# Layer norm sums all on VectorE in PSUM, four squares in flight, half of the float32 modulated tiles of 512 columns in a PSUM bank

## The chip, the cores and the metric

The kernel runs on one core of a Trainium2 chip. A core has five engines with queues of their own: TensorE (PE in the profile, its weight loads PEld), VectorE (DVE), ScalarE (ACT), GpSimd (POOL) and SyncE (SP, here only for DMAs). Each engine works through its queue in order. Data lies in SBUF, and in PSUM, which has eight banks of 512 float32 columns on 128 partitions; the engines that compute here read and write both, but GpSimd works on SBUF alone in this kernel. The metric is the time of one execution in device microseconds (us). Less is better.

## The reference

A two-layer backbone over 512 latent tokens and 256 context tokens of width 1024. Each layer is a half SwiGLU feed-forward, a mixer (neighbourhood attention in layer 0, windowed attention in layer 1) and a second half SwiGLU. Each of these sub-layers is modulated at its input and closed by a layer norm:

```python
def layer_norm(x, g, b):
    xf = x.astype(jnp.float32)
    mu = jnp.mean(xf, axis=-1, keepdims=True)
    var = jnp.mean(jnp.square(xf - mu), axis=-1, keepdims=True)
    return ((xf - mu) * lax.rsqrt(var + LN_EPS)).astype(x.dtype) * g + b

def modulate(h, shift, scale):
    return h * (1.0 + scale) + shift

def ffn_sublayer(h, shift, scale, gate, w_in, w_out, g, b):
    y = swiglu(modulate(h, shift, scale), w_in, w_out)
    return layer_norm(ALPHA * h + FFN_RES * gate * y, g, b)
```

## The kernel before

**Layout.** The hidden state lies transposed: the 1024 features are eight tiles `z[d]` of 128 partitions, the tokens are columns (0 to 511 latent, 512 to 767 context). A mean over features is then a sum over the eight tiles and over partitions.

**Precision.** Every float32 operand of the large matmuls is split into a high part and a rest (`uh`, `ul` for the modulated state, `wh`, `wl` for weights, `gh`, `gl` for the gated activations), and each product is three matmuls (`mm3`, lines 146 to 148). ACT rounds the weights to `wh` (line 102), POOL subtracts to get `wl` (line 104).

**Order.** The program is written as a sequence of tile operations. A planner orders each engine's queue by modelled times (`schedule_with_timeline_sim=True`), finds the dependencies between tiles, and hands out buffers: a tile with a tag takes one of the tag's `bufs` slots when its last user has finished. So PE's queue is a mixture of stages, and a matmul that stands in the queue ahead of others holds them back if its operand is late.

**PSUM.** `banks` gives the eight banks out by tag: "mm", "s" and "c" two each, "t" and "o" one each.

**Layer norm.** `layer_norm` (line 385) handles one group of columns, 256 or 512 wide. The groups are named by their key and place: l0_0 and l0_1, l2_0 and l2_1, l3_0 and l3_1 (each time 512 latent columns, then 256 context columns), l1_0, l1_1, l1_2 (256 each), l4_0, l4_1 (256 each), fin_0 (256). The last group of the program, fin_1, uses `layer_norm_pe`, which sums by matmuls. The steps of `layer_norm` are:

1. Sum of the eight tiles (`total` as `as..`): POOL adds tiles 0 to 3 into a SBUF tile, three adds; DVE adds tiles 4 to 6 into `part`, then POOL's sum, then tile 7, four adds.
2. A matmul with a matrix of 1/1024 sums over partitions and gives the mean `pm` to every partition (line 393).
3. DVE centers each tile in place (`center`, line 333), ACT squares it (line 398). Squares 0 to 2 are summed on POOL (two adds), square 3 is written to `part`, and DVE adds 4 to 7 and POOL's sum (five adds). Squares that don't start a sum go to the tag "ln" with two buffers.
4. Matmuls give the variance `pv` (line 404), eleven small DVE operations give its inverse root (`rstd`), a matmul spreads it over partitions (`spread`, line 356).

`pm`, `pv` and `spread` use one bank tag. `part` is the second half of `pm`'s own bank for a group of 256 columns, and the bank "t" for a group of 512.

**After the norm.** `ln_mod` multiplies each tile by the inverse root (line 411) and calls `mod_out`, which makes the modulated tile in float32 (`uf`, line 287, ACT), its high part (`uh`, line 289 on ACT or line 291 on DVE) and the rest (`ul`, line 292, DVE). For 512 columns `uf` takes one of the twelve "slab" buffers, which also hold weights and attention operands. `keep` (lines 299 and 305, POOL) then scales the tile for the residual. Group l3_0 reads and writes through a rearranged view of the columns (`rm`).

**Feed-forward tail.** `ffn` runs its chunks so that the latent group `a` is finished first. In the last chunk (`ci == NCH - 1`) come the products of `a`, then those of group `b` and the layer norm of `a` (`post(0)`), then `down` of `b`; the chunk marked "r" repeats the one before for `b` alone, with another `down` of `b`. `down` (line 466) makes eight products `pd` of six matmuls each, and DVE accumulates each into `z` (`accumulate`, line 432). In the tail `down` takes its banks from "sst" in turn: two of "s" and the one of "t".

Of the kernel before, what the change touches and what calls it, by code (L numbers as in the profile page):

```python
# [8 lines left out]
F32 = mybir.dt.float32  # L9
# [9 lines left out]
P = 128  # L19
D = 1024  # L20
DT = D // P
# [5 lines left out]
NCH = NF // 2  # L27
# [4 lines left out]
SLABS = 12  # L32
# [6 lines left out]
def hybrid_kernel(ctx: ExitStack, tc: tile.TileContext, h0, cc, crow, wmod, wmodt, bmod, lnp, wst,  # L39
                  rpbp, nmask, sinks, ropec, rmat, ident, wmask, out):  # L40
    nc = tc.nc
# [8 lines left out]
    def bank(tag, nm):  # L50
        return pp.tile([P, 512], F32, tag=tag, name=nm, bufs=banks[tag])

    def t2(nm, tag="t2"):
        return tp.tile([P, 512], F32, tag=tag, name=nm, bufs={"t2": 6, "ln": 2, "sl": 2}[tag])
# [28 lines left out]
    def zt(d, c0, c1):  # L83
        return zl[d][:, c0:c1] if c1 <= NL else z[d][:, c0:c1]
# [24 lines left out]
    ph, phase_of = {}, [None, ExitStack()]  # L109
# [159 lines left out]
    def mod_out(nm, d, c0, c1, st, prm, rm=False, dd=None):  # L269

        sc, bi, ag, ab = prm
        dd = d if dd is None else dd
        n = c1 - c0
        zs = zt(d, c0, c1)
        s1, s2 = sc[:, dd, st:st + 1], bi[:, dd, st:st + 1]
        if nm == "in":
            uf = t2(f"uf{nm}_{d}", "ln" if d < 3 else "t2")
        elif nm == "l0_1":
            uf = gp.tile([P, 256], F32, tag="gs", name=f"uf{nm}_{d}", bufs=6)
        elif n <= 256:  # L280
            uf = ph["S"].tile([P, 256], F32, tag="v", name=f"uf{nm}_{d}", bufs=9)
        else:
            uf = ph["S"].tile([P, 512], F32, tag="slab", name=f"uf{nm}_{d}", bufs=SLABS)
        uo, uv, lo, zv = uh[d][:, c0:c1], uf[:, :n], ul[d][:, c0:c1], zs
        if rm:
            uo, uv, lo, zv = rowm(uo), rows(uv), rowm(lo), rows(zs)
        nc.scalar.activation(uf[:, :n], zs, AF.Identity, scale=s1, bias=s2)  # L287
        if d in (1, 2, 4, 5, 7):
            hi = nc.scalar.activation(uo, zv, AF.Identity, scale=s1, bias=s2)
        else:  # L290
            hi = nc.vector.tensor_scalar(out=uo, in0=zv, scalar1=s1, scalar2=s2, op0=ALU.mult, op1=ALU.add)  # L291
        return hi, nc.vector.tensor_tensor(out=lo, in0=uv, in1=uo.bitcast(F32), op=ALU.subtract)  # L292
# [23 lines left out]
    def add(eng, out, a, b):  # L316
        behind(eng.tensor_tensor(out=out, in0=a, in1=b, op=ALU.add), last_rstd[0])
# [18 lines left out]
    def total(nm, n, src, split, part):  # L336


        accs = [t2(f"{nm}_{i}")[:, :n] for i in range(2)]
        a = src(0, accs[0])  # L340
        for d in range(1, split):
            add(nc.gpsimd, accs[0], a, src(d, None))
            a = accs[0]
        a = src(split, part)
        for d in range(split + 1, DT):
            if d == DT - 1:
                add(nc.vector, part, a, accs[0])
            add(nc.vector, accs[1] if d == DT - 1 else part, a, src(d, None))
            a = part
        return accs[1]  # L350

    def spread(nm, y, n, tag):

# [31 lines left out]
    def layer_norm(nm, c0, c1, tag):  # L385

        n = c1 - c0
        nj = n // P
        bk = bank(tag, f"pm{nm}")
        pm = bk[:, 0:n]  # L390
        part = bk[:, 256:256 + n] if n <= 256 else bank("t", f"pp{nm}")[:]
        acc = total(f"as{nm}", n, lambda d, acc: zt(d, c0, c1), 4, part)
        nc.tensor.matmul(pm, onesd[:], acc, start=True, stop=True)

        def square(d, acc):
            zs = center(d, c0, c1, pm)
            sq = acc if acc is not None else t2(f"sq{nm}_{d}", "ln")[:, :n]
            nc.scalar.activation(sq, zs, AF.Square)
            return sq

        acc = total(f"aq{nm}", n, square, 3, part)
        pv = bank(tag, f"pv{nm}")
        for j in range(nj):
            x = nc.tensor.matmul(pv[:, j:j + 1], acc[:, j * P:(j + 1) * P], onesd[:, 0:1], start=True, stop=True)
            behind(x, prev_ln[0])
        ve = pv[:, 8:8 + nj]
        nc.vector.tensor_scalar(out=ve, in0=pv[:, :nj], scalar1=EPS, scalar2=None, op0=ALU.add)
        pr, prev_ln[0] = spread(nm, rstd(nm, ve, nj, pv[:, 16:16 + nj]), n, tag)

        def norm(d):  # L410
            return nc.vector.tensor_tensor(out=zt(d, c0, c1), in0=zt(d, c0, c1), in1=pr, op=ALU.mult)  # L411
        return norm
# [23 lines left out]
    def ffn(nm, groups, gt, mid, post, units=(), opened={}, head=None, apart=None):  # L436
# [25 lines left out]
        def next_bank(nm):  # L462
            turn[0] += 1
            return bank(("mm", "s", "c")[turn[0] % 3], nm)

        def down(w, ci, gs, g, spread):
            c0, c1, st = g
            for d in range(DT):
                pn = f"pd{nm}_{ci}_{c0}_{d}"
                pd = (next_bank(pn) if spread else bank("sst"[d % 3], pn))[:, :c1 - c0]  # L470
                for i in range(2):
                    mm3(pd, rw(w, i, d * P, (d + 1) * P), [t[:, c0:c1] for t in gs[i]], i == 0, i == 1)
                accumulate(pd, d, c0, c1, st, gts[0])
# [134 lines left out]
        for ci in list(range(NCH)) + [("r", NCH - 2)]:  # L608
            r = isinstance(ci, tuple)
            if not r and 0 < ci < NCH - 2:  # L610
                phase("T")
                pace[0] = each * weight[ci] / (4 if ci < s0 else 14)
                if ci == s0 - 1:
                    saved = sums()
            if not r and s0 <= ci < NCH - 2:
                gs = [[gp.tile([P, NT], F32R, tag="gs", name=f"g{x}{nm}_{ci}_{i}", bufs=6) for x in "hl"] for i in range(2)]

                def lagging(ci=ci, gs=gs, u=wpos[0] + 2):
                    w = wunit(again=u, adding=True)
                    if ci == NCH - 3:  # L620
                        restore(saved)
                    for g in ([(0, NL, 0)] if nb == 2 else groups):
                        down(w, f"{ci}", gs, g, True)

                for i in range(2):
                    seven(f"{nm}_{ci}_{i}", wpos[0] + i, *gs[i])
                    while i == 0 and late_downs:
                        late_downs.pop()()
                late_downs.append(lagging)
                wpos[0] += 3  # L630
                if ci == NCH - 3:
                    late_downs.pop()()
                if ci == NCH - 3:
                    pace[0] = 1
                    while bg:
                        tick()
                continue
            if ci == NCH - 2:
                phase("S")
            late = ci == NCH - 2  # L640
            if late:
                again = wpos[0]
            w = [wunit(again=again + i) if r else unit(i == 2 and (ci == NCH - 1 or ci == 0 and apart is not None)) for i in range(3)]
            cn = f"r{ci[1]}" if r else f"{ci}"
            gs = [[gp.tile([P, NT], F32R, tag="gs", name=f"g{x}{nm}_{cn}_{i}", bufs=6) for x in "hl"] for i in range(2)]

            def avs(*todo):
                for g, i in todo:
                    av(w[i], f"{cn}_{i}", g, *gs[i], opened.get((i, g)) if ci == 0 else None, 4 if late else 0)
                    if not r and 0 < ci < s0:  # L650
                        tick()

            def dn(g):
                down(w[2], cn, gs, g, not r and 0 < ci < NCH - 2)

            a, b = groups
            if r:
                avs((b, 0), (b, 1))
                dn(b)
                post(1)  # L660
            elif late:
                avs((a, 0), (a, 1))
                dn(a)
            elif ci == NCH - 1:
                avs((a, 0), (a, 1))
                dn(a)
                avs((b, 0), (b, 1))
                post(0)
                dn(b)
            elif ci == 0 and apart:  # L670
                apart()
                avs((head[0], 0), (head[0], 1))
                dn(head[0])
                avs(*[(g, i) for g in head[1:] for i in range(2)])
                for g in head[1:]:
                    dn(g)
            else:
                avs(*([(g, i) for g in head for i in range(2)] if ci == 0 else [(a, 0), (b, 0), (a, 1), (b, 1)]))
                dn(a)
                dn(b)  # L680
            if ci == s0 - 1:
                fourth()
            if mid is not None and ci == 1:
                bias_tables()
# [626 lines left out]
```

## Time and profile before

| what | us |
|---|---|
| median of three runs | 2865.42 |
| lowest and highest of them | 2860.72, 2865.66 |
| the profiled execution's own time | 2863.12 |
| its span, first to last instruction | 2861.0 |

The mean granted clock of TensorE over the span is 0.977. The queries used are: the page (busy time of each engine), the list of waits (engine and line that waited, for whom, total us, times, longest), the order of time of one engine (start and length in us, engine, line, operation, output and inputs, shapes, and in brackets the idle time before it and what ended it), the groups of equal instructions (busy us, mean ns of one, idle time before them), the list of one source line, and a table of stretches with each engine's busy time. Lengths of matmuls overlap, since they are pipelined. A wait for several things is put down to the one that came last.

### The profile page before, as it was taken

What the parts mean: (1) busy time and instruction counts of PE and PEld (TensorE: products, weight loads), DVE (VectorE), ACT (ScalarE), POOL (GpSimd) and SP (SyncE); (2) the same over time, 40 slices, a digit from 0 to 9 for tenths busy, and PEclk for the clock granted to TensorE, in tenths of its full rate; (3) what the DMA queues carried; (4) which work ended last, traced back from release to release, by engine and by line L of the source; (5) the groups of instructions that cost most, each with busy time, mean ns of one, the idle gap of its engine ahead of it and who ended that gap; (6) DMA issues with size and microseconds to landing.
All of it is one profiled execution on the core that took longest, in us unless ns stands there. A gap on an engine that the chain in (4) does not pass through costs nothing. (4 is left out here: it accounts for less than half of the span.)

```text
span 2861.0 us, 48069 instructions
## 1 busy us (share of the span) xinstructions
PE 2716.4 (95%) x17122; PEld 2438.8 (85%) x17122; DVE 1820.9 (64%) x4122; ACT 1218.0 (43%) x2496; POOL 1675.4 (59%) x1488
## 2 busy tenths in 40 slices
PE   8999999999999979999999889999997999899997
PEld 5789999888888868899998779999886777789997
DVE  3597776375555677766553886666457767787744
ACT  4224433266446343333433424433336655444543
POOL 4547674475434445876644667676456545577763
PEclk9999999999999989999999999999999999999998
DMA  8465656232221213445452335656431111135562
GB/s 300 124 192 159 159 144 162 79 99 78 56 56 54 66 49 93 118 126 137 116 140 77 93 107 142 169 169 181 133 97 47 51 38 45 56 88 134 126 174 70
DMA packets 285871, 322.15 MB, mean 113 GB/s; under 512 B 28480, under 2 KB 174016, under 8 KB 284608
## 3 DMA queue, kind: packets, MB, share of 16 engines
q1 hardware_dynamic: 269792, 290.63, 34.5%
q0 software_dynamic: 15552, 28.32, 6.0%
q8 instruction: 135, 2.21, 0.3%
q14 instruction: 104, 0.85, 0.1%
q10 hardware_dynamic: 288, 0.14, 0.0%
HBM read 311.14 MB, written 12.25 MB: 113 GB/s over the span
## 5 line engine op out<-in xcount | busy, mean ns | idle before, releaser
L104 POOL TENSOR_TENSOR wl<-wr,wh 128x512 fp32r<-128x512 f32 x308 | 406.0, 1333 | 307.7 <-ACT wh L102 268.8
L104 POOL TENSOR_TENSOR wl_s<-S,wh_s 128x512 fp32r<-128x512 f32 x202 | 270.4, 1374 | 49.5 <-ACT wh_s L102 44.1
L102 ACT CAST wh<-wr 128x512 fp32r<-128x512 f32 x308 | 187.7, 621 | 228.6 <-DMA wr<-in_wst_dram 59.4
L102 ACT CAST wh_s<-S 128x512 fp32r<-128x512 f32 x216 | 132.1, 622 | 325.2 <-POOL S L541 80.9
L541 POOL TENSOR_TENSOR S<-wr,wr 128x512 f32<-128x512 f32 x108 | 147.5, 1366 | 172.7 <-DMA wr<-in_wst_dram 147.7
L198 DVE CUSTOM_DVE_ANT_0 jk<-wt,cb 128x512 f32<-128x512 f32 x278 | 185.3, 680 | 57.8 <-DMA wt<-in_wmodt_dram 56.2
L104 POOL TENSOR_TENSOR wl_a<-wr,wh_a 128x512 fp32r<-128x512 f32 x120 | 159.2, 1382 | 31.8 <-ACT wh_a L102 22.3
L102 ACT CAST wh_a<-wr 128x512 fp32r<-128x512 f32 x162 | 100.8, 623 | 133.5 <-PE pd1b L147 17.0
L432 DVE SCALAR_TENSOR_TENSOR z<-pd0b,gt,z 128x256 f32<-128x256 f32 (+1 forms) x176 | 102.7, 602 | 63.1 <-PE pd0b L148 62.9
L432 DVE SCALAR_TENSOR_TENSOR z<-pd1a,gt,z 128x512 f32<-128x512 f32 (+1 forms) x168 | 99.0, 620 | 41.1 <-PE pd1a L148 40.8
L432 DVE SCALAR_TENSOR_TENSOR z<-pd0a,gt,z 128x512 f32<-128x512 f32 (+1 forms) x168 | 98.0, 619 | 34.4 <-PE pd0a L148 34.2
L765 POOL TENSOR_SCALAR p<-p,l 128x512 f32<-128x512 f32 x64 | 44.3, 694 | 119.4 <-DVE l L863 111.0
L305 POOL TENSOR_SCALAR z<-z,ag_None,ab_None 128x256 f32<-128x256 f32 (+1 forms) x78 | 68.8, 888 | 67.0 <-DVE uh L291 65.3
L198 DVE CUSTOM_DVE_ANT_0 jk<-zspare,cb 128x512 f32<-128x512 f32 x138 | 92.7, 680 | 13.6 <-DMA zspare<-in_wmodt_dram 13.4
L765 POOL TENSOR_SCALAR pw<-pw,l 128x512 f32<-128x512 f32 (+1 forms) x64 | 40.9, 641 | 66.2 <-DVE l L1052 25.4
L541 POOL TENSOR_TENSOR S<-S,wr 128x512 f32<-128x512 f32 x54 | 77.2, 1430 | 4.2 <-DVE x0b L524 1.7
L541 POOL TENSOR_TENSOR S<-wr,S 128x512 f32<-128x512 f32 x54 | 76.5, 1416 | 4.0 <-DVE ul L526 0.6
L862 ACT ACTIVATE p<-s,m 128x512 f32<-128x512 f32 x64 | 44.1, 690 | 77.7 <-DVE m L860 72.7
L287 ACT ACTIVATE ufl<-z,bi_None,sc_None 128x256 f32<-128x256 f32 (+1 forms) x86 | 54.5, 657 | 34.3 <-DVE z L411 33.9
L432 DVE SCALAR_TENSOR_TENSOR z<-pd1b,gt,z 128x512 f32<-128x512 f32 (+1 forms) x98 | 56.5, 610 | 13.2 <-PE pd1b L148 11.0
L292 DVE TENSOR_TENSOR ul<-ufl,uh 128x256 fp32r<-128x256 f32 (+1 forms) x88 | 60.4, 696 | 0.9 <-ACT ufl L287 0.6
L146 PE MATMUL pd0a<-gh0a,wh 128*128 128x512 f32 (+1 forms) x144 | 50.3, 358 | 8.0 <-DVE z L432 7.8
(1462 smaller groups left out, 10701.1 us busy)
## 6 DMA issues: line engine op xcount, KB each, us to landing
wr<-in_wst_dram SPq DMA_DIRECT2D x524, 256.0 KB
wt<-in_wmodt_dram SPq DMA_DIRECT2D x160, 256.0 KB
zspare<-in_wmodt_dram SPq DMA_DIRECT2D x80, 256.0 KB
wr_0b<-in_wst_dram SPq DMA_DIRECT2D x42, 256.0 KB
wr_1b<-in_wst_dram SPq DMA_DIRECT2D x42, 256.0 KB
wr_2b<-in_wst_dram SPq DMA_DIRECT2D x42, 256.0 KB
wr_3b<-in_wst_dram SPq DMA_DIRECT2D x42, 256.0 KB
wm<-in_wmod_dram SPq DMA_DIRECT2D x8, 1024.0 KB
```

The source lines that it names most:

```text
L102: nc.scalar.copy(hi[:], src[:])
L104: eng.tensor_tensor(out=lo[:], in0=src[:], in1=hi[:].bitcast(F32), op=ALU.subtract)
L146: nc.tensor.matmul(ps, a[0], b[0], start=first, stop=False)
L198: x = nc.vector.tensor_tensor_reduce(out=junk[:], in0=w[:], in1=cb[st], scale=1.0, scalar=0.0, op0=ALU.mult, op1=ALU.add, accum_out=acc[:, ...
L287: nc.scalar.activation(uf[:, :n], zs, AF.Identity, scale=s1, bias=s2)
L292: return hi, nc.vector.tensor_tensor(out=lo, in0=uv, in1=uo.bitcast(F32), op=ALU.subtract)
L305: nc.gpsimd.tensor_scalar(out=zs, in0=zs, scalar1=prm[2][:, d:d + 1], scalar2=prm[3][:, d:d + 1], op0=ALU.mult, op1=ALU.add)
L432: last[0] = nc.vector.scalar_tensor_tensor(out=zt(d, c0, c1), in0=pd, scalar=gt[:, d, st:st + 1], in1=zt(d, c0, c1), op0=ALU.mult, op1=ALU ...
L541: nc.gpsimd.tensor_tensor(out=t[:], in0=a[:], in1=b[:], op=o)
L765: nc.gpsimd.tensor_scalar(out=p, in0=p, scalar1=r, scalar2=0.0, op0=ALU.mult, op1=ALU.add)
L862: last_exp[0] = nc.scalar.activation(p[:], ps[:], AF.Exp, bias=m[:, 0:1], scale=-1.0, accum_out=l[:, 0:1])
```

## The change

Four edits.

- `total` takes a `split` of 0: then POOL has no part, and DVE adds all eight terms, the running sum in `part`. The sum of tiles does so for groups of 256 columns (512 columns keep four tiles on POOL), the sum of squares for all groups.
- Squares lie differently: for 256 columns two of them share one "ln" tile, for 512 columns the even ones take a "t2" tile, so four can exist at a time.
- `mod_out` puts the float32 modulated tile of even `d`, for 512 columns, into the bank "t" instead of a slab (odd ones stay in a slab).
- `down` in the tail for group `b` (and in "r") uses the two "s" banks alone.

```diff
@@ mod_out
+        elif d % 2:
+            uf = ph["S"].tile([P, 512], F32, tag="slab", name=f"uf{nm}_{d}", bufs=SLABS)
         else:
-            uf = ph["S"].tile([P, 512], F32, tag="slab", name=f"uf{nm}_{d}", bufs=SLABS)
+            uf = bank("t", f"uf{nm}_{d}")
@@ total
-        accs = [t2(f"{nm}_{i}")[:, :n] for i in range(2)]
-        a = src(0, accs[0])
-        for d in range(1, split):
-            add(nc.gpsimd, accs[0], a, src(d, None))
-            a = accs[0]
+        if split:
+            pool = t2(f"{nm}_p")[:, :n]
+            a = src(0, pool)
+            for d in range(1, split):
+                add(nc.gpsimd, pool, a, src(d, None))
+                a = pool
+        res = t2(f"{nm}_r")[:, :n]
         a = src(split, part)
         for d in range(split + 1, DT):
-            if d == DT - 1:
-                add(nc.vector, part, a, accs[0])
-            add(nc.vector, accs[1] if d == DT - 1 else part, a, src(d, None))
+            if d == DT - 1 and split:
+                add(nc.vector, part, a, pool)
+            add(nc.vector, res if d == DT - 1 else part, a, src(d, None))
             a = part
-        return accs[1]
+        return res
@@ layer_norm
-        acc = total(f"as{nm}", n, lambda d, acc: zt(d, c0, c1), 4, part)
+        acc = total(f"as{nm}", n, lambda d, acc: zt(d, c0, c1), 4 if n > 256 else 0, part)
         nc.tensor.matmul(pm, onesd[:], acc, start=True, stop=True)
+        sqs = []
 
         def square(d, acc):
             zs = center(d, c0, c1, pm)
-            sq = acc if acc is not None else t2(f"sq{nm}_{d}", "ln")[:, :n]
+            if acc is not None:
+                sq = acc
+            elif n > 256:
+                sq = t2(f"sq{nm}_{d}", "ln" if d % 2 else "t2")[:]
+            else:
+                if d % 2:
+                    sqs.append(t2(f"sq{nm}_{d}", "ln"))
+                sq = sqs[-1][:, d % 2 * 256:d % 2 * 256 + n]
             nc.scalar.activation(sq, zs, AF.Square)
             return sq
 
-        acc = total(f"aq{nm}", n, square, 3, part)
+        acc = total(f"aq{nm}", n, square, 0, part)
@@ ffn, down
-        def down(w, ci, gs, g, spread):
+        def down(w, ci, gs, g, spread, tail=False):
...
-                pd = (next_bank(pn) if spread else bank("sst"[d % 3], pn))[:, :c1 - c0]
+                pd = (next_bank(pn) if spread else bank("sst"[d % (2 if tail else 3)], pn))[:, :c1 - c0]
@@ ffn, dn
-                down(w[2], cn, gs, g, not r and 0 < ci < NCH - 2)
+                down(w[2], cn, gs, g, not r and 0 < ci < NCH - 2, r or ci == NCH - 1 and g == b)
```

## The prediction

> **What bounds the kernel now.** I read the page first, then the list of who waited for whom on PE, then the order of time of all engines around each layer norm.
>
> ```profile
> span 2861.0 us, 48069 instructions
> PE 2716.4 (95%) x17122; PEld 2438.8 (85%) x17122; DVE 1820.9 (64%) x4122; ACT 1218.0 (43%) x2496; POOL 1675.4 (59%) x1488
> ```
>
> PE is busy for 2716.4 of 2861.0 us, and the change leaves PE's work as it is. A gain or a loss can therefore only lie in the 145 us in which PE has nothing. The waits of PE (us in total, times, longest) say what belongs to the layer norms:
>
> ```profile
> PE pvl L404 <- DVE aql L317: 25.1, 5, 11.7
> PE prl L356 <- DVE yl L328: 11.9, 6, 2.5
> ```
>
> The largest is PE waiting for `aq`, the summed squares: 25.1 us in five waits. The change leaves the rstd steps behind the 11.9 us alone. PE's order of time shows the five, each with its wait in brackets. They are groups l1_0, l1_1, l2_1, l3_1 and l4_0, all of 256 columns; the three sums of 512 columns are never waited for.
>
> ```profile
> 1028.81 1.02 PE L404 MATMUL pvl<-onesd,aql 128*128 128x1 f32 x4 [11.67 <-DVE aql L317]
> 1048.96 0.61 PE L404 MATMUL pvl<-onesd,aql 128*128 128x1 f32 x4 [0.25 <-DVE aql L317]
> 1617.36 1.02 PE L404 MATMUL pvl<-onesd,aql 128*128 128x1 f32 x4 [3.54 <-DVE aql L317]
> 2178.50 0.61 PE L404 MATMUL pvl<-onesd,aql 128*128 128x1 f32 x4 [4.34 <-DVE aql L317]
> 2451.27 1.01 PE L404 MATMUL pvl<-onesd,aql 128*128 128x1 f32 x4 [5.29 <-DVE aql L317]
> ```
>
> So the question is whether the sum of squares of a 256-column group gets shorter. Here is its order of time in l3_1, where nothing else is in the way: DVE's rows (L333 centers, L317 adds), then ACT's squares.
>
> ```profile
> 2168.71 1.42 DVE L333 TENSOR_TENSOR z<-z,pml 128x256 f32<-128x256 f32 x4 [0.19 <-PE pml L393]
> 2170.58 0.42 DVE L333 TENSOR_TENSOR z<-z,pml 128x256 f32<-128x256 f32 x1 [0.46 <-ACT pml L398]
> 2173.18 0.43 DVE L317 TENSOR_TENSOR pml<-pml,sql 128x256 f32<-128x256 f32 x1 [2.18 <-ACT sql L398]
> 2173.65 0.42 DVE L333 TENSOR_TENSOR z<-z,pml 128x256 f32<-128x256 f32 x1
> 2174.62 0.43 DVE L317 TENSOR_TENSOR pml<-pml,sql 128x256 f32<-128x256 f32 x1 [0.54 <-ACT sql L398]
> ...
> 2178.02 0.42 DVE L317 TENSOR_TENSOR aql<-pml,sql 128x256 f32<-128x256 f32 x1 [0.54 <-ACT sql L398]
> ```
>
> ```profile
> 2169.16 0.42 ACT L398 ACTIVATE aql<-z 128x256 f32<-128x256 f32 x1 [0.47 <-DVE z L333]
> 2169.49 0.75 ACT L398 ACTIVATE sql<-z 128x256 f32<-128x256 f32 x2
> 2170.16 0.39 ACT L398 ACTIVATE pml<-z 128x256 f32<-128x256 f32 x1
> 2172.73 0.42 ACT L398 ACTIVATE sql<-z 128x256 f32<-128x256 f32 x1 [2.18 <-POOL aql L317]
> ```
>
> Two things cost time. First, square 4 waits for POOL to release its buffer. Second, from the square that goes into `part` on, the centers no longer run ahead: center 4 waits for the square written into `part` (the row at 2170.58), and each later center stands behind the add before it, though DVE idles. Center, square, add, next center is a **round** of 1.44 us (add at 2173.18, next add at 2174.62). In a 256-column group `pm` and `part` are two halves of one PSUM bank. A 512-column group has them in two banks, and there the fifth center does not wait for that square: in l0_0, DVE runs six centers in a row while ACT still writes it.
>
> ```profile
> 571.91 3.67 DVE L333 TENSOR_TENSOR z<-z,pml 128x512 f32<-128x512 f32 x6
> ```
>
> ```profile
> 573.23 0.60 ACT L398 ACTIVATE ppl<-z 128x512 f32<-128x512 f32 x1
> ```
>
> I conclude that a center, which reads the bank, is ordered against every square and add that writes it. The totals of the two waits, in DVE's list at L333 and ACT's at L398:
>
> ```profile
>   ACT pml L398: 3.7, 3
> ```
>
> ```profile
>   POOL aql L317: 4.4, 2
> ```
>
> By the Trainium skill, PSUM — Partial Sum Buffer, section "PSUM bank collisions raise a hardware error", PSUM is to be guarded by bank and quadrant and not by address; the 3.7 us of waits agree. By that rule the sum below stands; without it rival 1 would.
>
> **The change part by part**, added to this execution's own time, 2863.1 us (its span, and 2.1 us around it). The median of the three runs before is 2865.4.
>
> *Squares of 256 columns.* Before, three squares go to SBUF and POOL, and four rounds follow, the last two with the add of POOL's sum between. After, square 0 goes straight into `part`, so center 1 waits for it, and all of adds 1 to 7 are rounds. Length after: 0.45 (center to square) + 0.39 + 7 x 1.44 = 10.9 us. Before, in l3_1: 2168.71 to 2178.44, 9.7 us, of which POOL's wait is about 1.7 (center 4 ends at 2171.00, its square starts at 2172.73). So without POOL's wait 8.0: the change **adds 2.9 us and removes POOL's wait**, which the 4.4 us say was there twice only, in l3_1 and here in l1_0:
>
> ```profile
> 1016.47 1.41 DVE L333 TENSOR_TENSOR z<-z,pml 128x256 f32<-128x256 f32 x4
> ...
> 1020.83 0.42 DVE L333 TENSOR_TENSOR z<-z,pml 128x256 f32<-128x256 f32 x1 [2.55 <-ACT pml L398]
> 1023.50 0.43 DVE L317 TENSOR_TENSOR pml<-pml,sql 128x256 f32<-128x256 f32 x1 [2.25 <-ACT sql L398]
> ```
>
> There it is 1.8 us (1021.25 to the square, which the add at 1023.50 follows by 0.45). Four squares in flight give a round nothing, since it holds one. Per group: l1_0 +1.1 (no other work for PE in its 11.67 us), l3_1 +1.2, l4_0 +2.9; l2_1 between 0 and +2.9, as PE's order can be filled with matmuls of the next stage, taken as +1.4; l1_1, l1_2 and l4_1, whose first rounds run beside the norms of the group before, between 0 and +2.9, nearer the 0.25 us of l1_1's wait: +0.5 each. l0_1 is covered by PE's own work. In fin_0 PE comes late (`aq` ends at 2822.6, `pv` starts at 2825.1), which covers 2.5 of the 2.9: +0.4.
>
> ```profile
> 2822.17 0.41 DVE L317 TENSOR_TENSOR aqfin<-pmfin,sqfin 128x256 f32<-128x256 f32 x1
> ```
>
> ```profile
> 2825.11 0.50 PE L404 MATMUL pvfin<-onesd,aqfin 128*128 128x1 f32 x4
> ```
>
> Together +8.5.
>
> *First sums of 256 columns.* Three adds leave POOL for DVE, 0.43 us each:
>
> ```profile
> L317 DVE TENSOR_TENSOR pml<-pml,z x8: 420/427/433, 606.6 to 2454.9; 128x256 f32<-128x256 f32 x8
> ```
>
> That is 1.3 us a group. It is hidden where the last `z` comes late, and not where DVE is the limit. The stretches from the norms of l1_0, l4_0, l3_0 and l0_0 on (length, busy time of PE, PEld, DVE, ACT and POOL, then the granted clock, DMA share and GB/s):
>
> ```profile
> 1033.00:1042.00 9.00, 7.82 (x46) 7.35 (x46) 8.97 (x26) 8.07 (x18) 6.40 (x9) 0.67 0.01 3
> 2456.00:2465.00 9.00, 8.01 (x45) 7.83 (x46) 9.00 (x26) 8.08 (x18) 6.95 (x10) 0.65 0.01 2
> 2142.00:2168.00 26.00, 19.02 (x140) 17.01 (x140) 25.82 (x33) 16.92 (x22) 25.28 (x16) 1.00 0.34 98
> 590.00:608.00 18.00, 17.64 (x97) 15.22 (x97) 17.98 (x30) 13.41 (x20) 16.75 (x15) 1.00 0.32 86
> ```
>
> DVE is full in all four, PE short of work in the first three. I take +1.0 for l3_1 and +0.6 each for l1_1 and l4_1 (half of 1.3): +2.2. The granted clock of 0.67 behind the long gap of l1_0 is taken to cost nothing, because DVE sets the pace there.
>
> *Squares of 512 columns.* Two POOL adds become two DVE adds, and the squares no longer wait for two buffers. No PE wait hangs on it: 0, from -1 to +1.
>
> *Half of the float32 modulated tiles in PSUM.* In l3_0 the subtraction L292 has two SBUF operands and takes 1602 ns; the norm L411, with one operand in PSUM, takes 673 for the same shape:
>
> ```profile
> L292 DVE TENSOR_TENSOR ul<-ufl,uh 128x512 fp32r<-128x512 f32 x8 | 12.8, 1602 | 0.0
> L411 DVE TENSOR_TENSOR z<-z,prl 128x512 f32<-128x512 f32 x8 | 5.3, 673 | 0.1
> ```
>
> Four tiles read from PSUM save between 0 and 4 x 0.93 = 3.7 us; since these reads are strided I take -2.5. In l0_0 and l2_0 PE's own work (17.64 of 18.00) hides it. By the Trainium skill, SBUF — State Buffer, section "Who interferes with whom", a VectorE instruction with two SBUF inputs contends with a GpSimd one that reads SBUF, and one with at most one such input does not. By that rule the four would fall all the way, 1.2 us more than I count.
>
> *Two banks for the tail's down products.* At the end PE runs three products ahead and then waits until DVE has done eight norms:
>
> ```profile
> 2830.28 0.28 PE L148 MATMUL pd1b_r<-gh1b_r,wl_1b 128*128 128x256 f32 x1
> 2832.72 0.39 PE L146 MATMUL pd1b_r<-gh1b_r,wh_1b 128*128 128x256 f32 x1 [2.17 <-DVE zspare L432]
> ```
>
> With two banks it is two products ahead: one product of six matmuls, 0.12 us apart, is done later: +0.7. The three other tails wait little now:
>
> ```profile
> PE pd1a_r L146 <- DVE z L432: 0.4, 1, 0.4
> ```
>
> Each may lose between 0 and 0.7 more; +0.4 together. POOL's saved time and the freed slabs: 0, no PE wait of the list is on POOL or on a slab; if that cover fails it is a gain.
>
> Sum: 8.5 + 2.2 - 2.5 + 1.1 = **+9.3**, so 2872.4 for this execution and 2874.7 from the median. I predict **2873 us**, slower by about 0.3%. The smallest difference that a measurement of this kernel can tell from none is about 0.2%, 5.7 us.
>
> **The rivals.**
>
> 1. *The centers run ahead after all* (chance 0.22). If the order of centers and adds were only the planner's choice, four squares in flight would leave DVE at 15 operations of about 0.42 us and 0.9 around them, 7.2 us instead of 9.7 (l3_1) or 12.4 (l1_0, 1016.47 to 1028.81). The long gaps would lose 5.2 in l1_0 and 2.5 in each of l2_1, l3_1 and l4_0 (l3_1's figure for all three): 12.7 us. With the other terms, +2.2, -2.5 and +1.1, the time is 2851. For it: the add could have been planned first. Against it: DVE idles 2.18 us with a center ready, and the wait at 1020.83 names ACT's write. It decides the sign as soon as centers precede adds in l1_0.
> 2. *It cancels* (0.25). The longer rounds of l2_1 and l3_1 are covered by next-stage matmuls (1.4 and 1.2 less), the shared groups cost nothing (1.5 less), PSUM reads give 3.7 (1.2 less): +4.0, 2867. For it: l0_1, l1_2 and l4_1 are missing from the five waits, so PE found other work there. Against it: in l1_0 and l4_0 PE had none, in 11.67 and 5.29 us.
> 3. *Two banks decide* (0.10). DVE is full while it does the tail's accumulates, and two banks tie PE to it. Each of the four feed-forward stages has two such groups of products. If each of the seven others loses 0.7 us, it is 4.9 instead of the 0.4: 2877. Against it: the 0.4 us.
>
> **How the numbers follow.** The forecast has 0.35, the rivals 0.22, 0.25 and 0.10; 0.08 is for a new order of the planner, 0.05 of it faster. Faster 0.27, within 0.2% 0.28, slower 0.45. The range runs from rival 1 with first sums at 0, 512 columns at -1 and PSUM reads at 3.7 (2851 - 2.2 - 1 - 1.2 = 2847) to rival 3 with l2_1 and the PSUM reads at their upper ends and the three shared groups half way up (2877 + 1.5 + 2.5 + 3.6, rounded up: 2886). The forecast's own range is 2868 to 2878.
>
> **What would show it.** In l3_1 and l4_0 DVE's rows would be center, center, add, center, add with adds 1.44 us apart, and center 0 to `aq` near 11 us; rival 1 would show centers in a row and about 7 us. ACT would no longer wait for POOL's `aq`. The wait before `pv` would be some 8 us in l4_0. L292 with the PSUM tile would take about 0.7 us. In the last tail PE would wait after two products. The prediction is wrong if the centers are free, or if PE's gaps before `pv` shrink.

## The result, and the profile after

The changed kernel takes 2896.6 us in the median of four runs (2891.7 to 2900.6); the kernel before, run beside it, took 2865.5. The ratio is 1.0104, its 95% interval 1.0084 to 1.0123: 31 us slower. The prediction was 2873, and its range ended at 2886. The direction was right, the size was not.

The head of the page of the changed kernel, as shown of the kernel before:

```profile
span 2898.9 us, 48006 instructions
PE 2725.0 (94%) x17122; PEld 2446.3 (84%) x17122; DVE 1836.8 (63%) x4173; ACT 1217.3 (42%) x2496; POOL 1625.6 (56%) x1437
```

PE executes the same 17122 matmuls. Its span less its busy time was 144.6 us and is now 173.9: 29.3 us more in which PE has nothing to do, of the 37.9 us by which this profiled execution's span is longer than the one before. The other 8.6 us are PE's own busy time, at a mean granted clock of 0.970 against 0.977. The list of PE's waits begins with:

```profile
PE pvl L416 <- DVE aql_r L319: 45.0, 7, 12.1
PE prl L360 <- DVE yl L330: 16.4, 7, 2.5
```

The wait for the summed squares grew from 25.1 us (five times) to 45.0 (seven times). The next table of stretches shows four of the five stages that hold layer norms, each cut from the first center of its first group to the last `ul` of its last: l1, l2, l3, l4 of the kernel before (length, then busy time of PE, PEld, DVE, ACT, POOL, then granted clock, DMA share and GB/s), and behind it the same of the changed kernel.

```profile
1016.50:1090.10 73.60, 51.47 (x340) 48.46 (x338) 55.88 (x161) 37.25 (x81) 37.58 (x45) 0.79 0.18 54
1566.20:1635.30 69.10, 60.55 (x381) 55.39 (x380) 56.46 (x123) 37.70 (x69) 46.70 (x41) 0.90 0.34 96
2122.60:2196.70 74.10, 60.28 (x390) 52.63 (x388) 61.22 (x121) 44.49 (x76) 56.27 (x44) 0.98 0.28 80
2441.00:2491.50 50.50, 39.21 (x281) 37.02 (x280) 42.35 (x119) 27.11 (x57) 27.27 (x31) 0.86 0.17 48
```

```profile
1019.80:1102.20 82.40, 52.67 (x335) 50.04 (x336) 62.28 (x171) 39.22 (x81) 27.97 (x32) 0.75 0.16 47
1579.70:1654.10 74.40, 59.94 (x379) 54.21 (x378) 58.33 (x130) 37.69 (x69) 37.23 (x34) 0.91 0.32 89
2144.30:2221.70 77.40, 61.90 (x390) 53.92 (x388) 58.34 (x128) 44.36 (x76) 47.58 (x37) 0.91 0.27 77
2468.10:2523.10 55.00, 38.19 (x264) 36.50 (x264) 44.75 (x125) 27.69 (x56) 20.61 (x23) 0.81 0.13 39
```

They grew by 8.8, 5.3, 3.3 and 4.5 us (the l0 stage, from 70.4 to 72.7, by 2.3): 24.2 of the 37.9 us. The other 13.7 us lie in the stretches between these stages. Part of them is the choice of execution: the one profiled here is the slowest of the four, 4.0 us above their median, and the one before is 2.4 us below its own. Such stretches also differ from kernel to kernel for no reason that an edit gives: the one between l2 and l3 takes 490.2 us here and 478.7 in e5 below, which differs from this kernel only in where running sums of the layer norms lie.

Here is l3_1, the group that the prediction showed, in DVE's order of time (L319 adds, L335 centers; start, length, in brackets the idle time and what ended it):

```profile
2185.93 0.41 DVE L319 TENSOR_TENSOR asl_r<-pml,z 128x256 f32<-128x256 f32 x1
2191.22 0.42 DVE L335 TENSOR_TENSOR z<-z,pml 128x256 f32<-128x256 f32 x1 [4.87 <-PE pml L397]
2192.09 0.42 DVE L335 TENSOR_TENSOR z<-z,pml 128x256 f32<-128x256 f32 x1 [0.45 <-ACT pml L410]
2192.99 0.43 DVE L319 TENSOR_TENSOR pml<-pml,sql 128x256 f32<-128x256 f32 x1 [0.48 <-ACT sql L410]
2193.46 0.42 DVE L335 TENSOR_TENSOR z<-z,pml 128x256 f32<-128x256 f32 x1
2194.37 0.43 DVE L319 TENSOR_TENSOR pml<-pml,sql 128x256 f32<-128x256 f32 x1 [0.48 <-ACT sql L410]
...
2201.34 0.42 DVE L319 TENSOR_TENSOR aql_r<-pml,sql 128x256 f32<-128x256 f32 x1 [0.54 <-ACT sql L410]
```

The rounds are there as predicted: center, center, then add and center in turn, adds 1.38 us apart, 10.5 us from center 0 to the end of `aq`. But look at the first two rows. The sum of tiles is ready at 2186.34, and the first center starts at 2191.22. In between DVE waits for PE, whose order of time has the reason:

```profile
2185.21 0.50 PE L146 MATMUL wk<-uh,wh 128*128 128x512 f32 x1
...
2190.58 0.59 PE L397 MATMUL pml<-asl_r,onesd 128*128 128x256 f32 x2
2190.83 0.58 PE L148 MATMUL wk<-uh,wl 128*128 128x512 f32 x1
2201.82 1.01 PE L416 MATMUL pvl<-onesd,aql_r 128*128 128x1 f32 x4 [10.41 <-DVE aql_r L319]
```

The planner has put 23 matmuls of the next product (`wk`) ahead of the matmul of the mean, and one behind it. So they run while DVE has nothing to do, and then PE waits 10.41 us for `aq`, with nothing left. In the kernel before, the matmul of the mean came first and the 24 `wk` matmuls filled the wait (4.34 us were left):

```profile
2168.00 0.67 PE L393 MATMUL pml<-asl,onesd 128*128 128x256 f32 x2 [0.15 <-DVE asl L317]
2168.32 0.58 PE L146 MATMUL wk<-uh,wh 128*128 128x512 f32 x1
...
2173.77 0.39 PE L148 MATMUL wk<-uh,wl 128*128 128x512 f32 x1
```

From the finished sum to that matmul it is now 2.1, 3.4, 4.0, 4.2 and 2.9 us in l1_1, l1_2, l2_1, l3_1 and l4_1; before it was 0.1, 0.5, 2.2, 0.1 and 0.1. The prediction has no such term.

### The profile page after: what moved, and what is told of

It reads as the page before. It is cut to its first block, busy times and chain, and to the rows that moved or that the text cites. A ratio compares the mean times of both kernels' runs of the same rounds, so it can differ in the third digit from the quotient of the medians.

```text
span 2898.9 us, 48006 instructions
## 1 busy us (share of the span) xinstructions
PE 2725.0 (94%) x17122; PEld 2446.3 (84%) x17122; DVE 1836.8 (63%) x4173; ACT 1217.3 (42%) x2496; POOL 1625.6 (56%) x1437
## 5 line engine op out<-in xcount | busy, mean ns | idle before, releaser
L444 DVE SCALAR_TENSOR_TENSOR z<-pd1a,gt,z 128x512 f32<-128x512 f32 (+1 forms) x168 | 99.1, 620 | 45.1 <-PE pd1a L148 44.9
L198 DVE CUSTOM_DVE_ANT_0 jk<-zspare,cb 128x512 f32<-128x512 f32 x138 | 92.6, 680 | 14.7 <-DMA zspare<-in_wmodt_dram 14.6
L146 PE MATMUL vn<-wh,uh 128*128 128x256 f32 x192 | 54.6, 284 | 0.0
```

The costliest lines, as they stand in the source:

```text
L146: nc.tensor.matmul(ps, a[0], b[0], start=first, stop=False)
L198: x = nc.vector.tensor_tensor_reduce(out=junk[:], in0=w[:], in1=cb[st], scale=1.0, scalar=0.0, op0=ALU.mult, op1=ALU.add, accum_out=acc[:, ...
L444: last[0] = nc.vector.scalar_tensor_tensor(out=zt(d, c0, c1), in0=pd, scalar=gt[:, d, st:st + 1], in1=zt(d, c0, c1), op0=ALU.mult, op1=ALU ...
```

## The experiments

Two questions: are the rounds really made by the shared bank, and why is the loss three times the forecast? The runs were made in batches, each with the kernel before beside it; a difference is from the median of that batch, an interval is of the ratio. "PE idle" is span less PE's busy time on the page of the one profiled execution.

| kernel | median us | from before | ratio (95%) | PE idle |
|---|---|---|---|---|
| before | 2865.5 | | | 144.6 |
| the change | 2896.6 | +31.1 | 1.0084 to 1.0123 | 173.9 |
| e1 squares of 256 columns alone | 2876.9 | +12.6 | 1.0027 to 1.0063 | 156.3 |
| e2 first sums of 256 columns alone | 2871.1 | +6.8 | 1.0005 to 1.0035 | 152.6 |
| e6 e1 and e2 together | 2893.0 | +27.5 | 1.0074 to 1.0130 | 176.9 |
| e4 squares of 512 columns alone | 2870.0 | +4.4 | 1.0001 to 1.0033 | 145.5 |
| e9 modulated tiles alone | 2893.1 | +25.1 | 1.0063 to 1.0100 | 164.8 |
| e10 tail's banks alone | 2860.1 | -8.0 | 0.9951 to 0.9981 | 142.2 |
| e3 tiles and tail | 2851.6 | -12.7 | 0.9943 to 0.9972 | 140.6 |
| e11 the change without tiles and tail | 2893.8 | +25.8 | 1.0071 to 1.0106 | 171.3 |
| e15 the change without the tiles | 2898.7 | +31.7 | 1.0100 to 1.0132 | 174.7 |
| e5 the change, running sum of squares in SBUF | 2854.3 | -10.0 | 0.9959 to 0.9986 | 137.1 |
| e8 before, running sum of squares in SBUF | 2853.9 | -11.7 | 0.9953 to 0.9983 | 136.9 |
| e7 e3, squares on VectorE, sum in SBUF | 2852.6 | -12.9 | 0.9940 to 0.9979 | 135.8 |
| e12 e3 and e8 | 2850.0 | -18.1 | 0.9919 to 0.9953 | 134.6 |
| e17 the change, mean first in l3_1 | 2883.1 | +17.8 | 1.0043 to 1.0084 | 159.6 |
| e13 the change, mean first in four groups | 2881.9 | +14.8 | 1.0037 to 1.0069 | 161.8 |
| e14 e2, mean first in four groups | 2877.9 | +10.9 | 1.0028 to 1.0058 | 159.9 |
| e16 before, mean first in four groups | 2861.7 | -3.6 | 0.9973 to 0.9998 | 145.9 |

### The parts, one at a time

**e1**: only the squares of 256 columns go over to VectorE, two to an "ln" tile.

```diff
-        acc = total(f"aq{nm}", n, square, 3, part)
+        acc = total(f"aq{nm}", n, square, 3 if n > 256 else 0, part)
```

> The kernel before with one part of the change alone: the squares of 256-column groups are summed by VectorE alone (square 0 straight into the PSUM half, two squares to one ln tile). Theory A (a center is ordered behind every square and add that writes its bank): seven rounds of about 1.4 us, center 0 to aq 10.5 to 12.7 us in l2_1, l3_1 and l4_0 (9.6, 9.7, 10.2 before), and +8 to +18 us in all, the waits before pv longer by 1 to 4 us each. Theory B (the loss of the change lies in the first sums, whose matmul PE now comes to late): the rounds cost little, within +-4 us of before.

Measured +12.6 us; l2_1, l3_1 and l4_0 take 12.7, 10.6 and 12.6 us from center 0 to `aq`, and 15.4 and 15.8 in l1_1 and l1_2 (12.5 and 10.7 before). The two POOL adds gone are no gain: the three rounds more outweigh them.

**e2**: only the first sums of 256 columns go over.

```diff
-        acc = total(f"as{nm}", n, lambda d, acc: zt(d, c0, c1), 4, part)
+        acc = total(f"as{nm}", n, lambda d, acc: zt(d, c0, c1), 4 if n > 256 else 0, part)
```

> The kernel before with the first sums of 256-column groups on VectorE alone, nothing else changed. Theory B: the matmul of the mean stands behind other matmuls in PE's queue, as in the changed kernel, where it starts 4.3 us after the sum is ready in l3_1 (0.1 before), 4.0 in l2_1 (2.2), 2.2 in l1_1 (0.0) and 2.8 in l4_1 (0.1); the time is +8 to +14 us. Theory A: only some 1 us of adds in each full stretch of VectorE, 0 to +4 us in all.

Measured +6.8, between the two expectations. The sums of squares are untouched, and even shorter (8.1 us in l3_1), but the matmul of the mean now runs 3.7 us after its sum in l3_1, 2.9 in l1_1, 2.0 in l1_2 and in l4_1, and l3_1's wait before the variance rises to 7.94 us. So the late matmul comes with this part.

**e6**: e1 and e2 together.

> The kernel before with both parts for 256 columns: first sums and squares on VectorE alone in the half of the mean's bank. Theory C (the longer rounds and the later matmul of the mean use up the same slack before pv, so together they cost more than the sum): +23 to +32 us, pv waits near 45 us in all. If they only add: +19 us.

Measured +27.5, as theory C expected, where the single ones add up to 19.4. The 8 us between are less than the joint uncertainty of the three runs, about 10 us. The waits before the variance are those of the change:

```profile
PE pvl L415 <- DVE aql_r L317: 45.3, 7, 12.0
```

They are 20.2 us above those of the kernel before; e1's are 11.3 above and e2's 6.1, together 17.4. The five layer norm stages as a whole grew by 14.6 us in e1, by 10.4 in e2 and by 25.7 in e6. So on the pages the two parts nearly add, and that they cost more together because they use up the same matmuls (theory C) is not shown.

**e4**: only the squares of 512 columns.

```diff
-        acc = total(f"aq{nm}", n, square, 3, part)
+        acc = total(f"aq{nm}", n, square, 0 if n > 256 else 3, part)
```

> The kernel before with the squares of the three 512-column groups summed by VectorE alone, even squares in t2 tiles; all else as before. If the parts simply add up, this one must bring what the first runs leave open: 31.1 - (12.6 + 6.8 - 12.7) = +24 us. My theory is that it brings far less, +2 to +7 us: center 0 to aq 12.9 us instead of 11.4, the norm 2 to 3 us later in each of three groups, where PE has other work, and that the rest of the change's loss comes from parts that take the same slack (next run).

Measured +4.4, against 0 in the prediction. No wait for the variance appears, but the sum takes 12.9 us instead of 11.4, and everything behind it is that much later; the interval only just excludes no difference.

### Tiles and tail

**e3** takes both edits alone, **e9** the tiles, **e10** the tail's banks.

```diff
+        elif d % 2:
+            uf = ph["S"].tile([P, 512], F32, tag="slab", name=f"uf{nm}_{d}", bufs=SLABS)
         else:
-            uf = ph["S"].tile([P, 512], F32, tag="slab", name=f"uf{nm}_{d}", bufs=SLABS)
+            uf = bank("t", f"uf{nm}_{d}")
...
-                pd = (next_bank(pn) if spread else bank("sst"[d % 3], pn))[:, :c1 - c0]
+                pd = (next_bank(pn) if spread else bank("sst"[d % (2 if tail else 3)], pn))[:, :c1 - c0]
```

> The kernel before with the even float32 modulated tiles of 512 columns in the t bank and the tail's down products in two banks, sums as before. If a subtraction with one operand in PSUM doesn't wait for GpSimd, norm 0 to the last ul in l3_0 falls from 24.9 us to about 17 and the time falls by 3 to 9 us. If the two banks tie PE to VectorE, PE waits for accumulates in the tails by 3 us or more in all and the time is the same or up to +5 us.

> The kernel before with the even modulated tiles of 512 columns in the bank tag t, the tail's banks as before. The two edits together took 12.7 us. Theory A (the subtraction that leaves the low part reads one operand from a bank and finishes sooner, so the last low part of each wide group comes earlier): all of the gain is here, 9 to 14 us under the kernel before, wide groups' time from the first normalised tile to the last low part down by 2 to 8 us. Rival B (the tail's banks gave it): within 3 us of the kernel before.

> The kernel before with the tail's products on two banks instead of three, tiles as before. Theory A: 0 to 3 us over the kernel before (the prediction had 1.1). Rival B: 9 to 14 us under it.

Together -12.7, more than expected. Alone, both expectations of e9 missed: the tiles cost 25 us. Both of e10 missed too: its -8.0 lies just short of the second. In e9 the stages that have such tiles grew, l0 by 9.6 us, l2 by 10.7 and l3 by 4.4; l1 and l4 stayed within 1.0. The third product of the tail wants bank "t", and there the four tiles now stand ahead of it. In l0 of e9 the last `ul` on DVE, then the first product on PE that goes on with the tail, and last the accumulates of the repeated chunk (least, median and longest ns, first and last start), which the next group waits for:

```profile
604.68 1.18 DVE L294 TENSOR_TENSOR ul<-ufl,uh 128x512 fp32r<-128x512 f32 x1 [1.35 <-ACT uh L291]
```

```profile
606.90 0.28 PE L146 MATMUL pd0a<-gh0a,wh 128*128 128x256 f32 x1
```

```profile
L434 DVE SCALAR_TENSOR_TENSOR z<-pd0a_r,gt,z x8: 467/479/484, 615.4 to 626.6; 128x256 f32<-128x256 f32 x8
```

In the kernel before the same eight run here:

```profile
L432 DVE SCALAR_TENSOR_TENSOR z<-pd0a_r,gt,z x8: 471/472/477, 591.2 to 602.9; 128x256 f32<-128x256 f32 x8
```

With the tail on the two "s" banks they come at 589.1 to 605.0 again (e3). So the tail's edit, which the prediction priced as a cost, is what makes the tiles bearable: it is worth 12.7 + 25.1 = 38 us once they are in "t". Beside that it takes 8 us off by itself, in no stage that the profiles would single out; why is open. What is left for the tiles, e3 less e10, is -4.7 us, uncertain by about 6.

**e11** puts both back in the changed kernel, **e15** only the tiles.

> The changed kernel with the modulated tiles and the tail's banks put back. If the gain of 12.7 us that these two parts made on the kernel before is also in the changed kernel, this one takes 2906 to 2912 us, 10 to 15 over the changed kernel. Rival: the waits for the variance take the gain up (PE comes sooner to a wait that ends when VectorE is done), and this kernel takes 2893 to 2900 us, as the changed kernel does.

> The changed kernel without the modulated tiles in PSUM, but with the tail on two banks. On the kernel before, the tail alone took 8 us off, the tiles alone added 25, and both together took 12.7 off; in the changed kernel both together made no difference that could be told. If the tail's gain is real and is its own, it is here too: 2884 to 2890 us. Rival (it is the order of the planner in one kernel, or the gain is taken up by the longer waits): 2892 to 2899 us.

2893.8 and 2898.7 against 2896.6: in the changed kernel neither the 12.7 nor the 8 us can be seen. Both times lie in the second expectation. But that longer waits before the variance take the gain up is not borne out: they come to 45.0 us in the changed kernel, 45.1 in e11 and 44.9 in e15. In the l3 stage the tiles still show (77.4 us with them, 79.5 in e15). Where the rest of the gain goes is open.

### The bank

**e5** is the change with one thing different: for 256 columns the running sum of squares is a SBUF tile instead of the second half of `pm`'s bank.

```diff
-        acc = total(f"aq{nm}", n, square, 0, part)
+        acc = total(f"aq{nm}", n, square, 0, part if n > 256 else t2(f"pq{nm}")[:, :n])
```

> The changed kernel, but the running sum of squares of a 256-column group lies in SBUF and not in the bank of the mean; nothing else differs. Theory A: the centers run ahead of the adds, center 0 to aq falls from 10.5-12.7 us to 7-8.5 us in l2_1, l3_1 and l4_0, the waits before pv shrink by 3 to 5 us each, and the time is 12 to 22 us below the changed kernel (1.002 to 1.006 of before). If the order were the planner's choice and not the bank's, the rounds stay and so does the time (1.010).

**e8** does the same to the kernel before (`3` instead of `0`).

> The kernel before with one difference: the running sum of squares of a 256-column group lies in an SBUF tile, not in the bank of the mean; GpSimd keeps its three squares. Theory A: the four rounds go, the centers run in a row, center 0 to aq falls from 9.6-10.2 us to about 7-8.5 us in l2_1 and l4_0, and the time falls by 3 to 9 us. GpSimd's adds stay in the way in l1_0 (square 4 waits for them). If the bank were not the cause: no change within +-3 us.

Measured against the kernel before, e5 is 41 us better than the changed kernel, about twice the upper end of what was expected: it takes 10 us less than the kernel before, and e8 takes 11.7 less. In the profiled executions the five layer norm stages have 26.9 us of e5's gain, and 20 us lie between them, where nothing was altered; that surplus is not explained. DVE's order of time in l3_1 of e5:

```profile
2156.70 2.74 DVE L335 TENSOR_TENSOR z<-z,pml 128x256 f32<-128x256 f32 x8 [4.85 <-PE pml L397]
2159.35 3.06 DVE L319 TENSOR_TENSOR pql<-pql,sql 128x256 f32<-128x256 f32 x6
2162.52 0.42 DVE L319 TENSOR_TENSOR aql_r<-pql,sql 128x256 f32<-128x256 f32 x1
```

Eight centers in a row, then the adds: 6.2 us in place of 10.5, with the same number of operations. The rounds came from the shared bank, not from the engines. (`pm` and `part` are also one tile of the program; no run separates tile and bank. The mean's matmul is still late here: 4.85 us of idle DVE.)

**e7** joins e3 with the squares of 256 columns on VectorE and the sum in SBUF; **e12** joins e3 and e8, where POOL keeps its three squares.

> The kernel before with float32 modulated tiles in the t bank and the tail's two banks, and the squares of 256-column groups summed by VectorE alone in an SBUF tile; first sums and the squares of 512 columns as before. Theory A: the gain of the tiles (-12.7 us) and that of short sums (6 to 8 us from center 0 to aq, pv waits 10 us less) both hold: 2838 to 2846 us, ratio 0.990 to 0.993. If short sums only hand the wait on to the next step: 2849 to 2853 us.

> The kernel before with the modulated tiles and tail of the change (alone 12.7 us under it) and the running sum of the squares of 256 columns in SBUF, GpSimd keeping its three squares (alone 11.7 us under it). If the two gains are in different places and add, 2838 to 2845 us. Rival: they use the same slack, as the other pair of this kind did, and it takes 2849 to 2855 us.

e7's first expectation missed, and its second held: it is no better than e3 alone, though its waits before the variance fell to 19.4 us from 26.7. e12's time lies in its second expectation, and its difference from the kernel before between the two: -18.1 us, where the gains add up to 24.4. It is the fastest version found, 0.6% under the kernel before and 1.6% under the changed one, though its interval overlaps that of e3.

### The place of the matmul of the mean

**e13** (the change) and **e14** (e2) order the products of the next stage behind that matmul in l1_1, l1_2, l3_1 and l4_1; **e17** does so in the change for l3_1 only; **e16** applies the rule of e13 to the kernel before, where those matmuls stand first already but for four in l1_2.

```diff
-        nc.tensor.matmul(pm, onesd[:], acc, start=True, stop=True)
+        pms[nm] = nc.tensor.matmul(pm, onesd[:], acc, start=True, stop=True)
...
+            hold[0] = pms["l3_1"]
             mmk(ps[:], w, i * P, 0, NL)
+            hold[0] = None
```

(`mm3` then puts each matmul behind `hold[0]` in PE's queue.)

> The changed kernel with one thing more: the products of the next stage are ordered behind the matmul of the mean in l1_1, l1_2, l3_1 and l4_1, as they are in the kernel before. Theory D (the place of that matmul in PE's queue is a cost of its own): the time from the finished sum of tiles to that matmul falls from 2.2, 3.4, 4.3 and 2.8 us to under 0.8 in the four groups, the wait before the variance in l3_1 falls from 10.4 to 5 to 7 us, in l1_1 from 4.6 to under 2, and the kernel takes 3 to 8 us less than the changed one (2896.6), 2889 to 2894. Rival: PE does the same matmuls in another place and waits as long in sum, now ahead of the matmul of the mean; within 2 us of the changed kernel.

> The kernel before with the first sums of 256 columns on VectorE only (alone 6.8 us over the kernel before) and the same ordering of PE's queue. Theory D: most of the 6.8 us is the late matmul of the mean; with it back in its place, 0 to 3 us over the kernel before, and l3_1's wait before the variance is 4 to 5 us instead of 7.9. Rival (the three more adds on VectorE are the cost): 5 to 9 us over it.

> The changed kernel with one place of PE's queue altered: in l3_1 the 23 matmuls of the next product that stand ahead of the matmul of the mean are ordered behind it. The rest of the order is as in the changed kernel. Theory D: the wait before the variance falls from 10.4 to 5 to 6 us, 1 to 1.5 us of waiting appears ahead of the matmul of the mean, and the kernel takes 3 to 5 us less than the changed one (2896.6): 2891.5 to 2893.5. Rival (the wait only changes its place): within 1.5 us of it.

> The kernel before with the same ordering rule in l1_1, l1_2, l3_1 and l4_1. There the matmuls of the mean stand ahead of the products already, but for four matmuls in l1_2, so the layer norms hardly change; what else moves is the planner's order in the stages behind. If a new order alone costs or gains, this kernel is 3 to 8 us away from the kernel before on either side, and the waits of the later feed-forward products for the second half of their operand differ from the 3.7 us of before. If not, it is within 2 us of it.

In e17, PE's order of time around l3_1 is now:

```profile
2175.70 0.67 PE L399 MATMUL pml<-asl_r,onesd 128*128 128x256 f32 x2 [1.39 <-DVE asl_r L321]
...
2187.02 1.01 PE L418 MATMUL pvl<-onesd,aql_r 128*128 128x1 f32 x4 [5.18 <-DVE aql_r L321]
```

10.41 us of waiting became 1.39 + 5.18, and the l3 stage takes 72.9 us in place of 77.4: 4.4 us, as theory D says for this place. The median fell by more, 13 us between the two differences from before, with intervals that just touch; the surplus isn't explained by that stage. The stretch between l2 and l3, where nothing was altered, is 4.8 us shorter in this execution as well.

The other places are no such gain. e13 is not measurably better than e17. In l1_1 and l4_1 PE now waits 5.2 us ahead of the matmul of the mean, since it may not begin with the matmuls that it did there before. And e14 fell against theory D: it was expected 0 to 3 us over the kernel before and is 10.9 over it, no better than e2 (+6.8). Its l3 stage gained 2.1 us (78.2 to 76.1), its l1 stage lost 3.3 (75.1 to 78.4). e16 is 3.6 us under the kernel before, its interval just clear of no difference, though the rule alters next to nothing in its layer norms; so a few us from such a rule may come from the planner's order elsewhere.

So the late matmul is a cost of its own where it spends all of the filling, as in l3_1, and elsewhere only another place for the same wait.

## Why the prediction was off

- **PE's gaps are the time: right in the main.** PE's idle time has 29.3 of the 37.9 us between the two profiled executions. Its busy time, which the prediction took as fixed, has the other 8.6.
- **The bank orders centers behind squares and adds: right, and shown, as far as bank and tile are one here.** Rounds of 1.38 us against 1.44, 10.5 us in l3_1 against 10.9; with the sum in another memory the rounds are gone (e5, e8). By the Trainium skill, PSUM — Partial Sum Buffer, section "PSUM bank collisions raise a hardware error", two engines at one bank and quadrant have to be ordered even if they touch different columns; the rounds agree. ACT waits for POOL's `aq` no more, and the wait in l4_0 is 8.80 us where some 8 were forecast. Rival 1 fell with this.
- **Squares of 256 columns, +8.5: too small.** Alone they cost 12.6 (e1). The term took l2_1 at half because matmuls of the next stage would fill it, and l1_1, l1_2 and l4_1 at 0.5 each. In e1 the waits of l2_1 and l1_1 are 6.70 and 3.66 us, where 3.54 and 0.25 were: there was little to fill them with.
- **First sums of 256 columns, +2.2: this step failed.** It counted three adds on DVE where DVE is the limit, and took the order of PE's queue as given. Alone they cost 6.8, and with them comes a matmul of the mean that stands behind other work: 4.4 us in l3_1 of the change (e17), and no cost that could be shown elsewhere. How the 6.8 divide between the adds and that place stays open, since e14 put the place right and showed no gain.
- **All sums together, 8.5 + 2.2 + 0 = 10.7: here the forecast failed.** They cost 25.8 (e11, the change without tiles and tail). The three parts alone add up to 23.8 (e1, e2, e4), so the loss is not in their meeting. Each term was too small, by 4.1, 4.6 and 4.4 us: the prediction halved or dropped costs because matmuls of PE would cover them, and too few did. For the squares of 256 columns the waits of e1 show it; the first sums have the late matmul besides; for the squares of 512 columns no wait shows where the time goes. Each part alone has an uncertainty of 4 to 5 us, about as much as it misses by; the sum of them is clear of the forecast.
- **Squares of 512 columns, 0: mis-sized.** 4.4 alone, with an interval that nearly reaches 0. No wait of PE hung on the sum, but what comes after it did.
- **Tiles in PSUM, -2.5: right in place, and in size as far as can be seen.** The l3 stage is 2.1 us shorter with the tiles in the changed kernel (e15 against it) and 3.5 in the kernel before (e10 against e3), each in one profiled execution; in the whole time the -4.7 are too uncertain to tell. L294 in l3_0, where even tiles lie in PSUM and odd ones in SBUF:

```profile
2170.79 0.68 DVE L294 TENSOR_TENSOR ul<-ufl,uh 128x512 fp32r<-128x512 f32 x1
2172.37 1.13 DVE L294 TENSOR_TENSOR ul<-ufl,uh 128x512 fp32r<-128x512 f32 x1
```

  The mean of the eight fell from 1602 to 910 ns. By the Trainium skill, SBUF — State Buffer, section "Who interferes with whom", one SBUF operand keeps a VectorE instruction clear of GpSimd; 0.68 us, as for the norm, agrees. Of the eight in l0_0 of the kernel before, three took 0.68 us with both operands in SBUF too, so an operand in the bank makes it no faster than that. Strided reads did not slow it: in l0_0 of the change, where they are not strided, it takes 0.68 to 0.69 us.
- **Two banks for the tail, +1.1: the wrong sign, and not seen as a condition.** The wait of the last tail, 2.2 us before, is 0.9 and 0.3 after. That tiles in "t" would block a tail that still uses "t" was missed; the tail's edit prevents it. Rival 3 fell.
- **Granted clock costs nothing: not settled.** In the stages l1, l3 and l4 it fell from 0.79, 0.98 and 0.86 to 0.75, 0.91 and 0.81, with the longer gaps; no run holds the gaps and changes the clock.

So the sums make 25.8 of the 31.1 us. Tiles and tail were to gain 1.4. They gain 12.7 without the new sums, and with them nothing that can be told from 0 (the 5.3 us that are left have an uncertainty of about 7). Why that gain is missing there stays open.

## What to carry to other kernels

Before moving work to an engine that has time, look whether the operands share a PSUM bank with something another engine writes: here the bank cost more than the engine, and with one running sum moved out of it the rewrite went from 31 us lost to 10 gained. Before halving a cost because other matmuls will cover it, count the matmuls that are left at that place. A reduction that one in-order engine finishes for another should be followed to its place in that engine's queue. An edit that looks like a small cost can be what keeps another edit from blocking; ask of each buffer that a change newly fills who else takes it in turn.

## What the runs showed of the hardware

The subtraction of a tile still in SBUF also got faster when its neighbours moved to PSUM: 1.09 to 1.17 us in l3_0 of the change, against a mean of 1.60 before. GpSimd's part of the work around it changed as well, so the cause is not singled out.
